# Attention's raw queries loaded six steps ahead of their rounding, into three buffers of their low parts

## The chip, the cores and the metric

The kernel runs on one core of a Trainium2 chip. The metric is device time in microseconds (us), the median of several runs. A core has five engines with instruction streams of their own: TensorE (PE, with its weight loads as PEld), VectorE (DVE), ScalarE (ACT), GpSimd (POOL) and SyncE (SP), which here issues nearly all DMA transfers. Each engine takes its instructions in the order in which they stand; semaphores make one wait for another.

## The reference, cut to what matters

One layer of a hybrid encoder over 2048 tokens (a 32 x 64 grid) and 16 meta tokens. An input projection feeds two mixers: neighbourhood attention (8 heads of 64, a window of 8 rows x 16 columns, a relative-position bias, 16 keys that all see) and a bidirectional gated DeltaNet (4 heads of 128, chunks). An output projection, a SwiGLU feed-forward and a norm follow.

```
s_grid = einsum('brqhd,brikhd->bhrqik', qg, k_win) + bias      # attention
s_meta = einsum('brqhd,bmhd->bhrqm', qg, km)
p      = softmax(concat([s_grid, s_meta]))
v_new  = u_i - w_i @ state                                     # DeltaNet, chunk by chunk
o_i    = q_i @ state + qk_i @ v_new
state  = state * cd_i + k_i^T @ v_new
h = h + concat([y_na, y_dn]) @ w_out;  h = h + (silu(u @ w_gate) * (u @ w_up)) @ w_down
```

## The kernel before

Phase A (up to about 880 us in the profile) projects and prepares; it writes queries, keys and values to DRAM scratch. Phase B (about 880 to 1300 us) runs attention and the DeltaNet scan side by side. Phase C does the output projection and the feed-forward, and PE is its limit.

Phase B is one loop over steps i (line 1322). A step of attention treats 128 queries of one head; four steps make a slot (32 slots, 128 steps). Beside it stands a step of the scan, `scan_a`, `scan_b`, `scan_c`, with one more scan step in each 16. In step i the code issues the transposes of i-1 (`att_t`, L1134), the scores of i+1 (`att_s`, L1120 and L1121), the values' load of i+4 (`att_v`, L1077) and the output of i-2 (`att_o`, L1148).

PE multiplies in a rounded form, so that a slot's queries are split: `load_q` (L1055) brings the raw queries (128 x 512, 256 KB, as two transfers of 64 partitions) into `qr`; `split` rounds them on ACT to `q1` (L1068), and POOL writes the rest `qr - q1` to `q2` (L1070). Both are multiplied with the keys. Slot n is first used by `att_s(4n)`, in step 4n-1. Its split is issued in step 4n-3 (`i % 4 == 1`). `qr` has one buffer, so the load, in step 4n-6 (`i % 4 == 2`), waits until POOL has finished the split of slot n-1, of step 4n-7. `q1` and `q2` have two buffers each.

What else SP loads in phase B: the bias `b` of a slot (L1062, in step 4n-5, two buffers, 336 to 672 KB), the scan's chunks `w<-dx` (L1179, 1 MB each) and `xq` (L1182, 512 KB), the keys `k` (L1047, 544 KB each), later the gates `z` (L1254) and the output weights `yu` (L1388). All are in one queue, q1. ACT also does the softmax (L1127), the copies `pT` of transposed scores (L1136) and the scan's `vn` (L1213 to L1217) and `oacc` (L1245), in one stream with the rounding of queries.

A scheduler sets each engine's order from the program, with times of its own for each instruction, and `tc.issue_after` holds the loads behind the last load of values. So an edit of a buffer count or of a step number moves instructions of other kinds as well.

Of the kernel before, what the change touches and what calls it, by code (L numbers as in the profile page):

```python
# [8 lines left out]
F32 = mybir.dt.float32  # L9
F32R = mybir.dt.float32r  # L10
# [6 lines left out]
P = 128  # L17
# [1001 lines left out]
def attention_slots():  # L1019

    slots = [Slot(2 * hp + a, [(C, 0, 4)]) for hp in range(3) for C in range(4) for a in range(2)]
    for R in (2, 0):
        slots += [Slot(6 + a, [(C, R, R + 2), (C + 1, R, R + 2)]) for C in (0, 2) for a in range(2)]
    return slots


def attention_loads(tc, S, es, rel):

    nc = tc.nc
    kp = es.enter_context(tc.tile_pool(name="b_k", bufs=2, reuse_waits="tile"))  # L1030
    vp = es.enter_context(tc.tile_pool(name="b_v", bufs=LV + 3, reuse_waits="tile"))
    A = Ctx()
    A.slots = attention_slots()
    A.kp, A.pools = kp, [kp, kp]
    A.tiles, A.last, A.keys = {}, None, {}

    def at(i):

        s = A.slots[i // 4]
        R, C, o = s.tiles[i % 4]  # L1040
        nch = 3 if CN[C] == 24 or R == 0 else 4
        return s, R, C, o, KWIN[R][0], KWIN[R][1], nch, KWIN[R][1] * CN[C] // nch

    def load_k(h):
        kk = A.pools[h % 3].tile([P, 34, 64], F32R, name=f"k{h % 3}", bufs=1)
        for l in range(2):
            nc.sync.dma_start(kk[l * 64:(l + 1) * 64].rearrange("p r c -> p (r c)").bitcast(F32), S.kx[h // 2, l, h % 2])  # L1047
        A.keys[h] = kk

    def load_q(n):  # L1050
        s = A.slots[n]
        s.qr = kp.tile([P, 512], F32, name="qr", bufs=1)
        C, R0, R1 = s.segs[0]
        for d in range(2):
            nc.sync.dma_start(s.qr[d * 64:(d + 1) * 64].rearrange("p (f n) -> p f n", f=len(s.segs)),  # L1055
                              S.qx[s.h, C:C + len(s.segs), :, R0 * P:R1 * P].rearrange("f d n -> d f n"))

    def load(n):
        s = A.slots[n]
        s.b = kp.tile([P, 1624], F32, name="b")  # L1060
        for o, src, n in s.bias:
            nc.sync.dma_start(s.b[:, o:o + n], rel[s.h, :, src:src + n])  # L1062

    def split(n):
        s = A.slots[n]
        s.q1 = kp.tile([P, 512], F32R, name="q1")
        s.q2 = kp.tile([P, 512], F32R, name="q2")
        nc.scalar.copy(s.q1, s.qr)  # L1068
        for c in (slice(0, 256), slice(256, 512)):
            nc.gpsimd.tensor_tensor(s.q2[:, c], s.qr[:, c], s.q1[:, c], ALU.subtract)  # L1070

    def load_v(i):
        s, R, C, o, k0, nr, nch, w = at(i)
        t = A.tiles[i] = Ctx()
        t.v = vp.tile([P, 4, 64], F32, name="v")
        src = S.vx[C][s.h].rearrange("r c d -> (r c) d")[k0 * CN[C]:(k0 + nr) * CN[C]]
        A.last = nc.sync.dma_start(t.v[0:w, 0:nch], src.rearrange("(p k) d -> p k d", k=nch))  # L1077

    A.at, A.load, A.load_q, A.load_k, A.split, A.v = at, load, load_q, load_k, split, load_v
    load_k(0)  # L1080
    load_q(0)
    load(0)
    split(0)
    load_v(0)
    return A


def phase_b(tc, S, A, W, norm_g, following):
# [4 lines left out]
    with ExitStack() as es:  # L1093
# [18 lines left out]
        def att_s(i):  # L1112
            s, R, C, o, k0, nr, nch, w = att_at(i)
            n = nch * w
            t = tiles[i]
            ps = pa_.tile([P, 512], F32, name="y")
            qs = slice(i % 4 * P, i % 4 * P + P)
            keys = A.keys[s.h][:, k0:k0 + nr, CLO[C]:CLO[C] + CN[C]]
            pv = ps[:, 0:n].rearrange("p (r c) -> p r c", r=nr)
            nc.tensor.matmul(pv, s.q1[:, qs], keys, start=True, stop=False)  # L1120
            nc.tensor.matmul(pv, s.q2[:, qs], keys, start=False, stop=True)  # L1121
            t.sb = ap_.tile([P, 512], F32, name="sb", bufs=3)
            t.mx = ap_.tile([P, 4], F32, name="mx", bufs=6)
            nc.vector.tensor_tensor_reduce(out=t.sb[:, 0:n], in0=ps[:, 0:n], in1=s.b[:, o:o + n], scale=1.0, scalar=-3.0e38,
                                           op0=ALU.add, op1=ALU.max, accum_out=t.mx[:, 0:1])
            nc.gpsimd.tensor_scalar(t.mx[:, 1:2], t.mx[:, 0:1], -1.0, None, op0=ALU.mult)
            nc.scalar.activation(t.sb[:, 0:n], t.sb[:, 0:n], AF.Exp, bias=t.mx[:, 1:2], accum_out=t.mx[:, 2:3])  # L1127

        def att_t(i):
            s, R, C, o, k0, nr, nch, w = att_at(i)  # L1130
            t = tiles[i]
            pt = pa_.tile([P, 4, P], F32, name="y")
            for c in range(nch):
                nc.tensor.transpose(pt[0:w, c], t.sb[:, c:nch * w:nch], S.ident)  # L1134
            t.pT = ap_.tile([P, 4, P], F32, name="pT", bufs=2)
            nc.scalar.copy(t.pT[0:w, 0:nch], pt[0:w, 0:nch])  # L1136
# [30 lines left out]
        def scan_load(s):  # L1167


            cs = (s, 15 - s)  # L1170
            new = [c for c in cs if c not in dxt]
            for c in new:
                dxt[c] = W.tile([P, 4, 4, P], F32, name="w")
            for d in range(2):
                xqt[d, cs[d]] = xp.tile([P, 4, 2, P], F32, name=f"xq{d}")
            for d, c in enumerate(cs):
                if c in new:
                    place[c] = (0, 1, 2, 3) if d == 0 else (3, 0, 1, 2)
                    nc.sync.dma_start(dxt[c], S.dx[c, :, :, d:d + 4].rearrange("h p a i -> p h a i"))  # L1179
                elif s != 8:  # L1180
                    nc.sync.dma_start(dxt[c][:, :, place[c][0]], S.dx[c, :, :, 4 * d].rearrange("h p i -> p h i"))
                nc.sync.dma_start(xqt[d, c], S.xq[d, c].rearrange("h p a i -> p h a i"))  # L1182
# [105 lines left out]
        nq = Pieces()  # L1288
        scan_load(0)
        A.load_q(1)  # L1290
        A.load_k(1)
        for i in range(1, LV):
            att_v(i)
# [2 lines left out]
        def scan_begin(j):  # L1296
            if j % 8 == 0 and j + 8 < N:
                with tc.issue_after(S.last.ins if j == 0 else A.last.ins):
                    scan_load(j // 8 + 1)
            if j < N:  # L1300
                scan_a(j)
# [15 lines left out]
        def scan_middle(j):  # L1317
            if 0 <= j - 1 < N:
                scan_b(j - 1)

        j = 0
        for i in range(N + 4):
            if i % 32 == 8 and i < 96:
                with tc.issue_after(A.last.ins):
                    A.load_k(i // 32 * 2 + 2)
            if i % 32 == 28 and i < 96:
                with tc.issue_after(A.last.ins):
                    A.load_k(i // 32 * 2 + 3)
            if (i == 0 or i % 4 == 3) and i < 120:
                with tc.issue_after(A.last.ins):  # L1330
                    A.load((i + 1) // 4 + 1)
            if i % 4 == 1 and i < 124:
                A.split(i // 4 + 1)
            if i % 4 == 2 and i < 120:
                with tc.issue_after(A.last.ins):
                    A.load_q(i // 4 + 2)
            extra = i % LEAD == LEAD - 1
            steps = list(range(j, min(j + 1 + extra, N + 2)))
            j = min(j + 1 + extra, N + 2)
            if 0 <= i - 1 < N:  # L1340
                att_t(i - 1)
            for k in steps[0:1]:
                scan_begin(k)
            if i + 1 < N:
                if min(j, N) - 5 in done:
                    with tc.issue_after(done[min(j, N) - 5].ins):
                        att_s(i + 1)
                else:
                    att_s(i + 1)
            if i + LV < N:  # L1350
                att_v(i + LV)
            for k in steps[0:1]:
                scan_middle(k)
            if 0 <= i - 2 < N:
                att_o(i - 2)
            for k in steps[0:1]:
                scan_end(k)
            for k in steps[1:]:
                scan_begin(k)
                scan_middle(k)  # L1360
                scan_end(k)
            nq.step(3 if j < N + 2 else 6)
            if i == SCANNED:
                assert j == N + 2
                nq.drain()
                es2.close()
                following()
# [538 lines left out]
```

## Time and profile before

| | us |
|---|---|
| median of 3 runs (lowest to highest) | 2893.03 (2889.85 to 2894.18) |
| the profiled execution's own time | 2883.66 |
| its span | 2881.9 |
| PE busy in the span | 2740.7 (95%) |
| phase B, about | 880 to 1300 |

PE is busy for 95% of the span, but not evenly: in phase A's end and in phase B it stands still now and then, and the clock granted to it (1.00 is 2.4 GHz, 0.50 is 1.2 GHz) falls in these places. The "busy" of PE is modelled at its ends; a bracket behind an instruction in the timeline gives the idle time just ahead of it and what ended it. A DMA share of 1.0 means that the 16 DMA engines are all occupied.

### The profile page before, as it was taken

The page shows a single profiled execution, that of the slowest core. Times are in us where ns is not written, and L with a number is a line of the kernel's source. Part 1 is how long each engine was busy: PE and PEld are TensorE (multiplying, and loading weights), DVE is VectorE, ACT ScalarE, POOL GpSimd, SP SyncE. Part 2 cuts the span into 40 slices and gives each one's busy share as a digit, 9 for nine tenths or more (in the row PEclk, how much of TensorE's full clock was granted, in tenths as well). Part 3 has the DMA queues.
Part 4 walks back from the last instruction along what each step waited for, and adds up shares of the span by engine and source line. Part 5 has one row for each costly group of instructions (what it writes and reads, how often), then busy time and mean ns, then how long its engine had stood idle before and what let it go on. Part 6 is the DMA issues. An engine that isn't in the chain of part 4 may idle for free.

```text
span 2881.9 us, 45992 instructions
## 1 busy us (share of the span) xinstructions
PE 2740.7 (95%) x16364; PEld 2400.2 (83%) x16364; DVE 1758.0 (61%) x3916; ACT 1170.4 (41%) x2741; POOL 744.4 (26%) x809
## 2 busy tenths in 40 slices
PE   8999988988988999979999999999999999999998
PEld 8999988988888988878887888877887888888886
DVE  5897467895643556764567566554548556654354
ACT  4652333652415667752334333243434333233342
POOL 2253353341511212221134322300104322220010
PEclk9999999999989999989999999999999999999999
DMA  4675654565769888985534222246353222225452
GB/s 151 189 205 142 163 165 135 172 179 172 211 159 287 265 229 254 291 281 156 176 126 163 81 88 80 81 131 246 128 176 119 80 86 88 74 95 201 143 179 70
DMA packets 385220, 462.15 MB, mean 160 GB/s; under 512 B 93492, under 2 KB 277133, under 8 KB 383423
## 3 DMA queue, kind: packets, MB, share of 16 engines
q1 hardware_dynamic: 383262, 452.92, 51.5%
q0 software_dynamic: 1728, 6.29, 0.6%
q8 instruction: 130, 2.13, 0.3%
q14 instruction: 100, 0.81, 0.1%
HBM read 329.95 MB, written 136.95 MB: 162 GB/s over the span
## 4 chain that ended last, share of the span: by engine, by line
PE 54%; DMA 3%; DVE 2%; ACT 0%; issue 0%; POOL 0%; SPq 0%; DVEq 0%; ACTq 0%; POOLq 0%
PE pg L1609 24%; PE pg L1685 8%; PE pd L1469 6%; PE pd L1685 4%; PE tp L1685 4%; PE pd L1609 4%; DMA rt<-ut 1%; DMA z<-zx 1%; PE y L1148 1%; DMA k<-kx 0%; PE tp L1495 0%; PE tp L1416 0%; DMA qr<-qx 0%; DVE w L1453 0%; PE y L1134 0%
## 5 line engine op out<-in xcount | busy, mean ns | idle before, releaser
L405 PE MATMUL acc<-uh,wf 128*128 128x384 f32 (+5 forms) x1920 | 469.2, 328 | 2.3 <-ACT uh L342 1.1
L1609 PE MATMUL pg<-T,w 128*128 128x512 f32 x1584 | 393.2, 397 | 2.6 <-ACT T L1452 1.4
L1453 DVE TENSOR_TENSOR w<-rw,w 128x512 fp32r<-128x512 f32 x308 | 241.1, 785 | 251.4 <-ACT w L1452 250.5
L1609 PE MATMUL pg<-B,w 128*128 128x512 f32 x1584 | 388.6, 398 | 3.6 <-ACT B L1452 3.0
L1452 ACT CAST w<-rw 128x512 fp32r<-128x512 f32 x308 | 190.2, 620 | 485.5 <-PE tp L1685 253.4
L1609 PEld LDWEIGHTS pg<-B,w 128*128 128x128 f32 x1584 | 299.1, 189 | 77.9 <-ACT B L1452 3.9
L1609 PEld LDWEIGHTS pg<-T,w 128*128 128x128 f32 x1584 | 298.0, 188 | 76.4 <-ACT T L1452 1.8
L405 PEld LDWEIGHTS acc<-uh,wf 128*128 128x128 f32 x1920 | 339.5, 192 | 4.9 <-ACT uh L342 1.2
L405 PE MATMUL acc<-ul,wf 128*128 128x384 f32 (+5 forms) x960 | 312.3, 325 | 0.0
L1557 POOL TENSOR_TENSOR s<-rw 128x512 f32<-128x512 f32 x88 | 120.4, 1369 | 548.0 <-DMA rw<-in_w_gate_dram 297.8
L1685 PE MATMUL pg<-w,hT 128*128 128x512 f32 x1056 | 260.8, 395 | 1.2 <-ACT hT L1452 1.1
L1685 PEld LDWEIGHTS pg<-w,hT 128*128 128x128 f32 x1056 | 198.1, 188 | 50.0 <-ACT hT L1452 1.5
L429 PE MATMUL acc<-wn,uh 128*128 128x256 f32 (+3 forms) x1056 | 210.7, 298 | 8.5 <-DVE vs L473 8.2
L1453 DVE TENSOR_TENSOR w<-s,w 128x512 fp32r<-128x512 f32 x176 | 131.6, 750 | 137.9 <-ACT w L1452 136.8
L1452 ACT CAST w<-s 128x512 fp32r<-128x512 f32 x176 | 108.5, 620 | 233.5 <-PE pg L1609 138.4
L405 PEld LDWEIGHTS acc<-ul,wf 128*128 128x128 f32 x960 | 184.3, 192 | 1.0 <-DVE ul L343 0.2
L429 PEld LDWEIGHTS acc<-wn,uh 128*128 128x128 f32 (+1 forms) x1056 | 173.3, 197 | 11.4 <-DVE vs L473 8.7
L429 PE MATMUL acc<-wn,ul 128*128 128x256 f32 (+3 forms) x528 | 158.0, 299 | 2.3 <-DVE rx_i L58 2.3
L1469 PE MATMUL pd<-w,yh 128*128 128x512 f32 x512 | 160.0, 394 | 0.0
L499 DVE SCALAR_TENSOR_TENSOR ct<-cr,cw,ct 128x1024 f32<-128x1024 f32 (+1 forms) x96 | 136.4, 1426 | 37.7 <-ACT ct L497 36.5
L242 POOL TENSOR_TENSOR wf<-raw,wf 128x512 fp32r<-128x512 f32 x80 | 117.7, 1486 | 154.9 <-ACT wf L241 131.6
L1623 DVE TENSOR_TENSOR eg<-pg,eg 128x512 f32<-128x512 f32 x110 | 75.9, 690 | 106.4 <-PE pg L1609 106.3
(359 smaller groups left out, 5305.0 us busy)
## 6 DMA issues: line engine op xcount, KB each, us to landing
rw<-in_w_down_dram SPq DMA_DIRECT2D x88, 512.0 KB
w<-dx SPq DMA_DIRECT2D x24, 1024.0 KB
rw<-in_w_gate_dram SPq DMA_DIRECT2D x44, 512.0 KB
rw<-in_w_up_dram SPq DMA_DIRECT2D x44, 512.0 KB
hd<-eg SPq DMA_DIRECT2D x88, 256.0 KB
s<-hd SPq DMA_DIRECT2D x88, 256.0 KB
raw<-in_w_feat_dram SPq DMA_DIRECT2D x80, 256.0 KB
xq<-xq SPq DMA_DIRECT2D x32, 512.0 KB
```

Of the source, the lines that this page charges most:

```text
L242: nc.gpsimd.tensor_tensor(lo, raw, hi, ALU.subtract)
L405: nc.tensor.matmul(ps[:, 0:c1 - c0], hl[:, a, k, :], (U.h, U.l)[l][ci][:, k, c0:c1], start=(i == 0), stop=(i == 23))
L429: nc.tensor.matmul(ps[0:np_, 0:n], (U.h, U.l)[l][ci][:, k, off:off + np_], hl[:, a, k, 0:n], start=(i == 0), stop=(i == 23))
L499: nc.vector.scalar_tensor_tensor(tt, raw[:, j:j + T], cw[:, b, j:j + 1], tt, op0=ALU.mult, op1=ALU.add)
L1148: nc.tensor.matmul(po, t.pT[0:w, c], t.v[0:w, c], start=(c == 0), stop=(c == nch - 1))
L1452: nc.scalar.copy(dst_h, src)
L1453: eng.tensor_tensor(dst_l, src, dst_h, ALU.subtract)
L1469: nc.tensor.matmul(ps, (yh, yl)[a][:, k], wo[k][:, b, cs], start=(i == 0), stop=(i == 23))
L1557: nc.gpsimd.tensor_tensor(s, p, q, op)
L1609: nc.tensor.matmul(ps, w[:, a, k], t[:, b, k], start=(k == 0 and (a, b) == (0, 0)), stop=(k == 3 and a == 1))
L1623: nc.vector.tensor_tensor(dst, ps, x0, ALU.add)
L1685: nc.tensor.matmul(acc[j][hf], hk[f][:, a, j * P:(j + 1) * P], wk[f][hf][:, b], start=(f == 0 and i == 0), stop=(f == NFF - 1 and i == 2))
```

## The change

`qr` loses its own buffer. The raw queries go to the buffer of the low parts, `q2`, which has three buffers in place of two (the memory stays the same), and POOL subtracts in place. The load of slot n moves from step 4n-6 to step 4n-9, six steps ahead of the split in place of three. It now waits until PE has made the last product with `q2` of slot n-3, `att_s(4n-9)`, issued in step 4n-10. Slot 2 is loaded before the loop as well.

```diff
     def load_q(n):
         s = A.slots[n]
-        s.qr = kp.tile([P, 512], F32, name="qr", bufs=1)
+        s.q2 = kp.tile([P, 512], F32R, name="q2", bufs=3)
+        s.qr = s.q2.bitcast(F32)
...
         s.q1 = kp.tile([P, 512], F32R, name="q1")
-        s.q2 = kp.tile([P, 512], F32R, name="q2")
         nc.scalar.copy(s.q1, s.qr)
...
         A.load_q(1)
+        A.load_q(2)
         A.load_k(1)
...
-            if i % 4 == 2 and i < 120:
+            if i % 4 == 3 and i < 116:
                 with tc.issue_after(A.last.ins):
-                    A.load_q(i // 4 + 2)
+                    A.load_q(i // 4 + 3)
```

SP's order around the fourth load of keys, before: `b` is the bias, `qr` the raw queries (the first here are slot 9's), `v` values, `k` keys, `w` and `xq` the scan's chunks.

```order
570 L1062 DMA b<-in_rel_dram 128x1008
571 L1077 DMA v<-vx_62 104x192
572 L1047 DMA k_11464<-kx 64x2176 x2
573 L1077 DMA v<-vx_59 96x192
574 L1077 DMA v<-vx_59 128x192
575 L1055 DMA qr<-qx 64x512 x2
576 L1077 DMA v<-vx_59 128x192
577 L1179 DMA w<-dx 128x4x512 x2
578 L1062 DMA b<-in_rel_dram 128x1008
579 L1077 DMA v<-vx_59 104x192
```

The same place now; `q` is the buffer of low parts that takes the raw queries of slots 10 and 11.

```order
569 L1056 DMA q_11418<-qx 64x512
570 L1063 DMA b<-in_rel_dram 128x1008
571 L1056 DMA q_11418<-qx 64x512
572 L1077 DMA v<-vx_62 104x192
573 L1047 DMA k_11459<-kx 64x2176 x2
574 L1077 DMA v<-vx_59 96x192
575 L1077 DMA v<-vx_59 128x192 x2
576 L1179 DMA w<-dx 128x4x512 x2
577 L1056 DMA q_11582<-qx 64x512
578 L1063 DMA b<-in_rel_dram 128x1008
579 L1056 DMA q_11582<-qx 64x512
```

The queries stand on both sides of a bias now, one slot and more ahead of where they stood; the keys, the values, the bias and the chunks keep their order among themselves.

ACT's order around the rounding of slot 4, before: the rounding stands behind the last exponential (128 x 416) ahead of its slot.

```order
687 L1136 COPY pT<-y 128x512
688 L1127 ACTIVATE sb,mx<-sb,mx 128x416
689 L1213 ACTIVATE vn<-z,kd 128x128
690 L1217 COPY vn<-z 128x128
691 L1068 CAST q_10799<-qr 128x512
692 L1136 COPY pT<-y 128x512
```

The same rounding now:

```order
669 L1217 COPY vn<-z 128x128
670 L1068 CAST q_10798<-q_10546 128x512
671 L1127 ACTIVATE sb,mx<-sb,mx 128x416
672 L1245 COPY oacc<-z 128x128
673 L1136 COPY pT<-y 128x512
674 L1213 ACTIVATE vn<-z,bkd 128x128
```

It stands five exponentials, so five steps of attention, further ahead. In most other slots the rounding stood as far ahead in the kernel before.

## Rows read from the trace of the kernel before

**Rows 1.** The page: span, busy time of each engine, the chunks' transfers
```profile
span 2881.9 us, 45992 instructions
PE 2740.7 (95%) x16364; PEld 2400.2 (83%) x16364; DVE 1758.0 (61%) x3916; ACT 1170.4 (41%) x2741; POOL 744.4 (26%) x809
...
w<-dx SPq DMA_DIRECT2D x24, 1024.0 KB
```

**Rows 2.** Windows: phase B, a quiet stretch, two parts of B
```profile
core 0: us, PE busy (x) PEld busy (x) DVE busy (x) ACT busy (x) POOL busy (x), PEclk, DMA share, GB/s
880.00:1300.00 420.00, 371.29 (x2826) 358.78 (x2825) 253.80 (x1038) 270.12 (x873) 93.73 (x221) 0.91 0.90 270
957.00:977.00 20.00, 20.00 (x173) 19.86 (x172) 10.80 (x46) 14.55 (x47) 4.31 (x12) 1.00 1.03 312
940.00:1180.00 240.00, 221.57 (x1779) 216.70 (x1778) 141.97 (x594) 161.56 (x534) 54.16 (x132) 0.95 0.87 251
1180.00:1256.00 76.00, 66.57 (x515) 63.55 (x513) 61.77 (x260) 57.69 (x191) 19.21 (x39) 0.93 1.02 321
```

**Rows 3.** Tile qr, 880 to 1300 us: who waited for it
```profile
  ACT q L1068: 51.1, 12
```

**Rows 4.** PE's timeline: three of seven stalls, and slot 25's first scores
```profile
930.00 0.69 PE L1120 MATMUL y<-k,q 128*128 128x384 f32 x1 [2.98 <-ACT q L1068]
983.36 0.80 PE L1232 MATMUL z<-S,w 128*128 128x128 f32 x2 [4.26 <-ACT vn L1217]
1195.88 0.67 PE L1120 MATMUL y<-k,q 128*128 128x384 f32 x1
1281.50 0.91 PE L1134 MATMUL y<-ident,sb 128*128 128x128 f32 x3 [6.19 <-ACT sb L1127]
```

**Rows 5.** ACT's timeline at two of these places
```profile
982.27 0.62 ACT L1068 CAST q<-qr 128x512 fp32r<-128x512 f32 x1 [4.44 <-DMA qr<-qx]
983.06 0.25 ACT L1217 COPY vn<-z 128x128 f32<-128x128 f32 x1
...
1193.33 0.62 ACT L1068 CAST q<-qr 128x512 fp32r<-128x512 f32 x1 [8.74 <-DMA qr<-qx]
```

**Rows 6.** Windows: the seven stretches from a stall to the clock's return
```profile
926.00:937.00 11.00, 8.02 (x42) 7.63 (x41) 3.27 (x11) 3.90 (x12) 1.83 (x4) 0.69 0.99 336
978.00:988.00 10.00, 5.74 (x31) 5.53 (x31) 2.80 (x13) 4.16 (x14) 1.80 (x4) 0.66 1.05 345
1020.00:1033.00 13.00, 7.87 (x43) 7.39 (x42) 2.95 (x12) 4.63 (x14) 1.76 (x4) 0.74 1.03 282
1079.00:1087.00 8.00, 4.16 (x23) 3.93 (x23) 2.52 (x12) 4.12 (x14) 1.60 (x3) 0.79 0.92 265
1115.00:1125.00 10.00, 6.83 (x34) 6.27 (x34) 4.21 (x18) 4.75 (x15) 1.74 (x4) 0.66 0.93 283
1186.00:1199.00 13.00, 7.18 (x36) 6.69 (x34) 6.35 (x21) 5.67 (x16) 3.21 (x6) 0.62 1.07 315
1275.00:1289.00 14.00, 7.81 (x41) 7.65 (x40) 6.21 (x20) 3.62 (x9) 6.22 (x11) 0.63 0.68 195
```

**Rows 7.** SP's timeline: loads of queries, chunks and bias
```profile
922.87 0.54 SPq L1062 DMA_DIRECT2D b<-in_rel_dram  x1
...
973.36 1.09 SPq L1055 DMA_DIRECT2D qr<-qx  x2
...
976.83 2.07 SPq L1179 DMA_DIRECT2D w<-dx  x2
...
1182.12 0.61 SPq L1055 DMA_DIRECT2D qr<-qx  x1
...
1188.91 0.33 SPq L1062 DMA_DIRECT2D b<-in_rel_dram  x1
```

**Rows 8.** SP's own waits, 840 to 1320 us
```profile
SPq L1062 <- DVE R L1201: 10.0, 10, 2.9
SPq L1055 <- POOL mx L1126: 4.7, 5, 2.0
```

**Rows 9.** DVE, 880 to 1300 us: the add of the bias, by line
```profile
L1124 DVE CUSTOM_DVE_ANT_0 sb<-y,b 128x384 f32<-128x384 f32 (+4 forms) x128 | 72.6, 570 | 26.8 <-PE y L1121 19.4 <-issue 3.6 <-POOL q L1070 0.9
```

## The prediction

> **What bounds the kernel now.** I read the page first: PE is busy for 2740.7 of 2881.9 us [rows 1]. So only stretches in which PE stands still, or runs at half clock, have anything to give, and I looked for those with the windows. In 880 to 1300 us PE is busy for 371.29 of 420 us at a mean clock of 0.91, while the DMA engines are at 0.90 of their time [rows 2]. This is where the queries are loaded; phase C behind it is bound by PE. Then the tile `qr`: inside these 420 us ACT waits 12 times, 51.1 us together, for the raw queries of a slot [rows 3]. Whether that reaches PE is seen on PE's own timeline. At 930.00 PE waits 2.98 us for the rounded queries themselves. At 983.36 it waits 4.26 us, and for the scan's `vn`, which has nothing to do with queries [rows 4]: ACT stood 4.44 us in front of the rounding at 982.27, and `vn` is behind it in ACT's stream [rows 5]. So a late query stops the softmax and the scan, steps before its slot is used. Seven such places stop PE: in slots 4, 9, 12, 17, 20, 25 and 31.
>
> Each costs more than its idle time. After it the granted clock is 0.50 for some microseconds, which is the level of 1.2 GHz. What a place costs is read from its window: length, less its matmuls divided by the rate of a quiet stretch, which is 173 in 20 us, or 8.65 in a us, at a clock of 1.00 [rows 2]. The seven windows [rows 6] give 11 - 42/8.65 = 6.1; 10 - 31/8.65 = 6.4; 13 - 43/8.65 = 8.0; 8 - 23/8.65 = 5.3; 10 - 34/8.65 = 6.1; 13 - 36/8.65 = 8.8; 14 - 41/8.65 = 9.3. Together 50.0 us. That is the whole of what earlier queries can bring here.
>
> **The change part by part.** *The load moves three steps ahead.* Phase B's 2826 matmuls over 128 steps are 22 to a step, and 22/8.65 = 2.5 us is a quiet step [rows 2], so the load gets some 7.6 us more. From the issue to the rounding it took 982.27 - 973.36 = 8.9 us in slot 9 and 1193.33 - 1182.12 = 11.2 us in slot 25 [rows 5, 7]; ACT had stood there for 4.44 and 8.74 us of these. Moved by 7.6 us, the first is in time with 3 us to spare, and the second is late by about 1 us. For slot 25 there is more: its load stood behind the keys, and now stands ahead of them, as the order around the fourth load of keys shows in another slot. So I count the waits for queries as gone, or small. In slot 4 the rounding itself has moved five exponentials ahead, so that there the added time is mostly taken back by an earlier deadline; its load, too, stands four loads of values further ahead in SP's order than it did, and I count it as in time.
>
> *The new wait.* The load now waits on SP for PE's product of slot n-3. Behind it on SP stand a bias, values and chunks, and PE and DVE wait for those. But the bias beside it waits for DVE's add in the same attention step 4n-9, which comes after that product. So the new wait ends first, and holds SP for no longer than it would be held: 0 us. The bias's own waits show the size, 10.0 us in 10 times [rows 8], none of them followed by a wait of DVE (below). The old wait, for POOL, goes: 4.7 us in 5 times, SP's alone, worth 0 by itself. If PE's product came after the bias's release, one step would be lost to all loads behind it; the price of that is a rival below.
>
> *Instructions.* The two loads, the rounding and the two subtractions remain, as many and as long. POOL now writes in the buffer that it reads; the trace has no row of that. The bounds are 0 and the time of one product of POOL that others wait for, and no engine but PE waits for it, a slot ahead: 0 taken. Three loads of 256 KB are under way or held where one was; bytes and buffers are the same in sum.
>
> *What is late next.* The queue is. In 880 to 1300 us it moved 270 GB/s x 420 us = 113.4 MB. With every engine occupied (1.03) it moved 312 GB/s, so those bytes take 363 us: 57 us less than now, for all of the phase. But the room isn't where the stalls are: 940 to 1180 us has 60.2 MB, 193 us at 312 GB/s, so 47 us free; 1180 to 1256 us ran at 321 GB/s and a share of 1.02 and has none [rows 2]. Four of the seven windows are full (shares of 0.99, 1.05, 1.03 and 1.07), three are not (0.92, 0.93, 0.68) [rows 6].
>
> The transfer that would be late next is the bias. It is issued four steps ahead of its use, about 10.2 us, and is larger than the queries. Its slack today is made by the stalls: in slot 4 it is issued at 922.87 and PE starts on the slot at 930.00, 7.1 us later; in slot 25 at 1188.91 and 1195.88, 7.0 us [rows 4, 7]. Queries took 8.9 to 11.2 us in a full queue. That no DVE add ever waits for a DMA [rows 9] says only that the queries were later still.
>
> The sum. Windows that aren't full: slots 17 and 20 in whole, 5.3 + 6.1 = 11.4. Slot 31 lies at the end of attention, where no scan is left to fill PE and the steps wait for each other; of its 9.3 I take two thirds, 6. The four full windows (6.1 + 6.4 + 8.0 + 8.8 = 29.3): between nothing (the bias takes over) and all, I take a third, 10, since two of them (slots 4 and 25) have a bias just behind and two (9 and 12) have a bias issued well before its use. 11.4 + 6 + 10 = 27 us. The profiled execution took 2883.66 us, so 2856 in its terms; it lies 9.4 us under the median of the runs shown, 2893.03, from which I take the 27: **2866 us**.
>
> The Trainium skill speaks for more: "DMA: Bandwidth & Descriptors", Specifications, puts HBM's limit for one core at about 358 GB/s. By that figure the 113.4 MB would need 317 us (an estimate of that page), the queue would be no limit, and all 50 us would come. The rows disagree, since 312 and 321 GB/s went with shares above 1.0 [rows 2]; I go by them.
>
> **The rivals.**
> *All of it comes:* 2893 - 50 = 2843. For it: every one of the seven stalls ends with a query, and no other transfer is seen to be waited for. Against it: the full queue in four of them.
>
> *The wait only changes its name:* with earlier queries the bias, the values or a chunk stops DVE and PE at the same places, and only the 11.4 us of slots 17 and 20 come, or half of it, since steps that run faster fill the queue there too: 2882 to 2887. For it: 7 us between issue and use of the bias in slots 4 and 25. Against it: in the other slots the bias has a step more than the queries had.
>
> *Slower:* the bias is late at the twelve pairs of chunks. The order shows two chunks of 1 MB (2.1 MB, 6.7 us at 312 GB/s) directly ahead of query, bias, query, so that a bias meets a full queue there. Queries took 8.9 to 11.2 us in a full queue, and a bias of 504 KB is 0.25 MB more, 0.8 us: some 10 to 12 us, up to 2 us after its use at 10.2. With the clock's loss, about 3 us in each of the seven windows (6.1 less 2.98 idle in the first), that is 5 us, and for the twelve pairs [rows 1] 60; less the 50 gained, 2903. It decides from a latency of the bias of 10.2 us on. Against it: the chunks stood directly ahead of a bias before as well [rows 7], and no add waited for one.
>
> *The change doesn't do what it says:* SP comes to the loads no sooner, since its place is set by the loads of values ahead of it, and the queries still arrive after ACT. The roundings stand up to five steps ahead of their use in ACT's stream, so a part of this is likely; all of it would be 2893. Against it: SP's order has them three loads of values further ahead.
>
> **How the numbers follow.** Forecast, around 2866: 0.50, its own range 2854 to 2879. All of it: 0.17. The wait changes its name: 0.16, half of it below the bound. Nothing comes: 0.08. Slower: 0.09. A measurement of this kernel tells about 0.2% from no change, 5.8 us. Faster: 0.50 + 0.17 + 0.11 = 0.78. Same: 0.05 + 0.08 = 0.13. Slower: 0.09. The range reaches to 2845, nearly to the whole of the gain, and to 2888, the end of the second rival; it leaves about 0.2 out, most of it on the slow side and below 2845.
>
> **What would show it.** In the profile of the changed kernel ACT's wait for the queries' transfer falls from 51 us to under 10; PE has no idle time of over 2 us for ACT's `vn`, `sb` or `oacc` behind a rounding between 940 and 1180 us; the clock's mean in phase B rises from 0.91 to 0.95 or more; the DMA rate of phase B rises from 270 to about 288 GB/s (113.4 MB in some 393 us); and DVE's add shows a DMA, the bias, among its releasers. If PE's stalls are gone and the bias is no releaser, the gain was cut too far; if ACT's wait stays above 30 us, the move of SP's loads was the wrong step; if the stalls stay with other names, the queue was the limit.

## The result, and the profile after

| | before | changed |
|---|---|---|
| median, us (lowest to highest) | 2891.44 (2888.75 to 2894.18) | 2866.62 (2864.26 to 2869.15) |
| ratio, 95% interval | | 0.9923 [0.9903, 0.9943] |
| the profiled execution | 2883.66 | 2866.91 |

The forecast was 2866. But the two profiled executions differ by only 16.75 us: that of before lay 7.8 us under its median, that of the change at its own. In a later comparison of the two the change stood at 2866.18 and 0.9927 [0.9903, 0.9951], the kernel before at 2886.15. So the change is worth 20 to 25 us.

The page, first lines, answering to [rows 1]; PE is busy for 9.9 us less:
```profile
span 2865.1 us, 46004 instructions
...
PE 2730.8 (95%) x16364; PEld 2391.9 (83%) x16364; DVE 1765.7 (62%) x3916; ACT 1170.9 (41%) x2741; POOL 742.8 (26%) x809
```

Windows of the changed kernel, three stretches of [rows 2] and a further one of 20 us (columns as there):
```profile
880.00:1300.00 420.00, 374.28 (x2904) 360.05 (x2903) 263.17 (x1057) 272.58 (x879) 92.83 (x220) 0.95 0.93 273
940.00:1180.00 240.00, 224.50 (x1825) 219.27 (x1825) 152.93 (x631) 164.61 (x546) 54.52 (x136) 0.97 0.95 267
1180.00:1256.00 76.00, 70.91 (x555) 68.33 (x554) 62.11 (x262) 62.62 (x202) 21.51 (x46) 0.96 1.02 332
1160.00:1180.00 20.00, 14.38 (x113) 13.29 (x112) 13.32 (x66) 9.85 (x34) 2.66 (x8) 0.99 1.04 238
```
The granted clock rose from 0.91 to 0.95, and between 940 and 1180 us the DMA share from 0.87 to 0.95: PE made 1825 products there in place of 1779, and the queue is fuller.

Tile `q`, who waited (the answer to [rows 3]: 51.1 us in 12 times):
```profile
  DMA q<-qx: 29.1, 11
```
The wait is smaller, not gone. PE's timeline, every stall of over 2 us from 900 us on (beside [rows 4]):
```profile
929.20 0.49 PE L1199 MATMUL z<-S,w 128*128 128x128 f32 x2 [2.23 <-ACT oacc L1245]
...
987.16 0.80 PE L1199 MATMUL z<-S,w 128*128 128x128 f32 x2 [4.47 <-ACT oacc L1245]
...
1088.05 0.91 PE L1134 MATMUL y<-ident,sb 128*128 128x128 f32 x3 [2.75 <-ACT sb L1127]
...
1177.76 0.85 PE L1148 MATMUL y<-v,pT 128*128 128x64 f32 x6 [2.92 <-DMA v<-vx]
...
1277.83 2.07 PE L1470 MATMUL pd<-w,yh 128*128 128x512 f32 x4 [13.74 <-ACT yh L1419]
```
Before there were seven, 29.8 us together; now there are four inside attention, 12.4 us, and a new one behind it, 13.74 us. ACT's timeline at the first, the second and the last:
```profile
928.36 0.62 ACT L1068 CAST q<-q 128x512 fp32r<-128x512 f32 x1 [5.72 <-DMA q<-qx]
...
986.32 0.62 ACT L1068 CAST q<-q 128x512 fp32r<-128x512 f32 x1 [6.52 <-DMA q<-qx]
986.84 0.26 ACT L1245 COPY oacc<-z 128x128 f32<-128x128 f32 x1
...
1277.19 1.07 ACT L1419 CAST yh<-tp 128x512 fp32r<-128x512 f32 x2 [16.28 <-DVE z L1281]
```
The first three lines are the picture of before again ([rows 5]): ACT stands in front of a rounding, and the scan's copy behind it is late for PE. The stall at 1088.05 is not of this kind, since no rounding waited there. POOL stood in front of the gates `z` of a norm; the softmax's `mx` came behind them, and ACT and PE waited for it:
```profile
1085.68 1.40 POOL L1256 TENSOR_TENSOR z<-z,ng 128x256 f32<-128x256 f32 x2 [5.65 <-DMA z<-zx]
...
1087.29 0.61 ACT L1127 ACTIVATE sb<-sb,mx 128x384 f32<-128x384 f32 x1 [3.54 <-POOL mx L1126]
```
And the one at 1177.76 waits for values. So two of the four stalls end with a query, one with gates, one with values. The four windows, by the measure of [rows 6]:
```profile
925.00:934.00 9.00, 6.77 (x43) 6.33 (x42) 2.77 (x10) 4.26 (x13) 1.83 (x4) 0.81 1.04 267
984.00:994.00 10.00, 6.84 (x39) 6.84 (x40) 3.37 (x14) 5.71 (x20) 1.82 (x4) 0.66 0.98 277
1084.00:1092.00 8.00, 5.25 (x30) 5.06 (x29) 2.10 (x9) 4.71 (x18) 4.73 (x9) 0.71 1.08 331
1174.00:1184.00 10.00, 7.03 (x45) 6.52 (x44) 3.11 (x14) 3.43 (x13) 1.58 (x3) 0.83 1.00 287
```
Length less matmuls by 8.65 is 4.0 + 5.5 + 4.5 + 4.8 = 18.8 us, against 50.0 before. So by this measure 31.2 us were gained inside attention, and 13.7 of idle time came behind it. The balance, 17.5, is near the 16.75 between the profiled executions. (The products behind the new wait are slow as well: the first eight output products take 4.3 us, 2.4 before, so that the loss is some 2 us more than the idle time.)

The loss: the last gates (norm of chunk pair 15), in the timelines of DVE, POOL and SP:
```profile
1273.53 3.57 DVE L1281 SCALAR_TENSOR_TENSOR z<-oacc,of,z 128x128 f32<-128x128 f32 x8 [9.94 <-POOL z L1256]
...
1272.78 1.40 POOL L1256 TENSOR_TENSOR z<-z,ng 128x256 f32<-128x256 f32 x2 [11.03 <-DMA yu<-yo]
...
1268.68 0.41 SPq L1254 DMA_DIRECT2D z<-zx  x1
...
1270.93 0.34 SPq L1254 DMA_DIRECT2D z<-zx  x1
```
PE's last product of attention starts at 1262.0 us, where it started at 1309.0 before. But the loads of the last `z` are issued at 1268.68 and 1270.93, since `z` has two buffers and SP has other loads ahead; POOL, DVE, ACT and PE follow one another from there, and the first output product starts at 1277.83 (1294.4 before), 17 us sooner. The 47 us are not like for like: before, the output products had begun ahead of attention's last 26 products and stood among them; now all of attention comes first.

Where did the longer lead go? SP's timeline at slot 10's load:
```profile
971.77 0.45 SPq L1056 DMA_DIRECT2D q<-qx  x1
973.93 0.35 SPq L1063 DMA_DIRECT2D b<-in_rel_dram  x1
976.20 0.45 SPq L1056 DMA_DIRECT2D q<-qx  x1
```
The second half goes out 4.4 us after the first, a bias between them, and 10.1 us ahead of the end of ACT's wait at 986.32. From the starts of all loads and roundings of slots 4 to 31 the medians are: from the second half's issue to the rounding 6.2 us before, 9.45 now; from the rounding to the slot's first scores 8.85 before, 12.35 now. So of the 7.6 us planned, the transfer got 3.3; 3.5 went to roundings that themselves stand further ahead. What SP waits for ahead of the queries' loads now (us, times, longest), 840 to 1320 us:
```profile
SPq L1056 <- DMA xq<-xq: 10.9, 6, 2.9
SPq L1056 <- DMA k<-kx: 6.2, 4, 2.1
SPq L1056 <- DMA b<-in_rel_dram: 5.8, 6, 2.0
SPq L1056 <- PE y L1121: 2.7, 5, 1.2
SPq L1056 <- POOL q L1070: 2.5, 4, 1.2
SPq L1056 <- POOL mx L1126: 2.2, 3, 1.3
```
The new wait for PE's product is the fourth line, and small. The last two say that SP still waits for POOL, 4.7 us as before [rows 8]; why, the record doesn't show. The first three are transfers still under way: all of SP's waits for a DMA, 880 to 1300 us, sum to 121.8 us (before 90.2).

DVE's add of the bias, the answer to [rows 9]:
```profile
L1124 DVE CUSTOM_DVE_ANT_0 sb<-y,b 128x384 f32<-128x384 f32 (+4 forms) x128 | 72.8, 570 | 22.4 <-PE y L1121 11.9 <-POOL q L1070 4.4 <-issue 3.6
```
The bias is not among the three releasers that the line names; the view of all waits has it once, with 0.5 us. The 4.4 us for POOL's `q` (0.9 before) are a single wait.

### The profile page after: what moved, and what is told of

The parts are those of the page before. It is cut to its first block, busy times and chain, and to the rows that moved or that the text cites. A ratio compares the mean times of both kernels' runs of the same rounds, so it can differ in the third digit from the quotient of the medians.

```text
span 2865.1 us, 46004 instructions
## 1 busy us (share of the span) xinstructions
PE 2730.8 (95%) x16364; PEld 2391.9 (83%) x16364; DVE 1765.7 (62%) x3916; ACT 1170.9 (41%) x2741; POOL 742.8 (26%) x809
## 4 chain that ended last, share of the span: by engine, by line
PE 69%; DMA 11%; DVE 10%; issue 4%; POOL 3%; ACT 2%; SPq 2%; DVEq 0%; POOLq 0%; ACTq 0%
PE pg L1610 25%; PE pg L1686 8%; PE pd L1470 6%; PE acc L405 5%; PE pd L1686 4%; PE tp L1686 4%; PE pd L1610 4%; PE acc L429 3%; DVE ct L499 2%; PE y L1148 2%; DMA q<-qx 1%; DMA w<-dx 1%; DMA xq<-xq 1%; DVE tl L166 1%; DVE yl L167 1%
## 5 line engine op out<-in xcount | busy, mean ns | idle before, releaser
L429 PEld LDWEIGHTS acc<-wn,uh 128*128 128x128 f32 (+1 forms) x1056 | 173.2, 197 | 13.7 <-DVE vs L473 10.8
L1470 PE MATMUL pd<-w,yh 128*128 128x512 f32 x512 | 161.2, 397 | 13.7 <-ACT yh L1419 13.7
```

The source lines that it names most:

```text
L429: nc.tensor.matmul(ps[0:np_, 0:n], (U.h, U.l)[l][ci][:, k, off:off + np_], hl[:, a, k, 0:n], start=(i == 0), stop=(i == 23))
L1470: nc.tensor.matmul(ps, (yh, yl)[a][:, k], wo[k][:, b, cs], start=(i == 0), stop=(i == 23))
```

## The experiments

Three theories stood against each other: the gain comes from the lead of the load; it comes from the buffers, which free the rounding and its place in ACT's order; and what remains is held by the queue's bytes or by its order. Times are compared with the kernel before in the same comparison: 2886.47 us for the first four, 2886.04 for the next four, 2886.15 for the last three.

**Buffers alone** (on the kernel before):
```diff
-        s.qr = kp.tile([P, 512], F32, name="qr", bufs=1)
+        s.q2 = kp.tile([P, 512], F32R, name="q2", bufs=3)
+        s.qr = s.q2.bitcast(F32)
...
-        s.q2 = kp.tile([P, 512], F32R, name="q2")
```


> The three shared buffers alone: the raw queries go into the buffer of the low parts, but are loaded in step 4n-6 as in the kernel before, three steps ahead of the rounding. Theory (the lead of the load is what pays): the load still has about 8 us to the rounding, ACT's wait for queries in phase B stays at 40 to 55 us, and the time is that of the kernel before, 2886 to 2893 us; only the start of phase B, where slot 1's load no longer waits for POOL, may give 2 to 3 us. Rival A (the second wait that went, for POOL's subtraction on one buffer, is what pays): ACT's wait falls to about 29 us as in the changed kernel and the time is about 2867 us. Rival B (any new order by the scheduler does it): somewhere between, with PE's stalls in other places but ACT's wait for queries not smaller.


Measured: 2874.68 us, 0.9957 [0.9940, 0.9973], 11.8 us less. In its trace:
```profile
ACT q L1068 <- DMA q<-qx: 35.3, 12, 5.8
```
The time lies between the theory's and rival A's, and ACT's wait, at 35.3 us, is smaller than the theory and rival B had it. About half of the gain comes without any step of lead, although PE waits ahead of the output products here already (9.79 us). The issue-to-rounding median is 6.7 us, hardly longer than before (6.2). What did change is the rounding's place: in the kernel before, eight slots (4, 5 and 25 to 30) are rounded less than 3 us ahead of their first scores, here two, in the changed kernel none. The load's wait for POOL is gone as well. Which of the two brings the 11.8 us was not separated: of the seven stalls before, only those of slots 4 and 25 had so late a rounding.

**Five steps instead of six** (on the changed kernel, slot 2 not loaded ahead of the loop):
```diff
-            if i % 4 == 3 and i < 116:
+            if i % 4 == 0 and i < 120:
                 with tc.issue_after(A.last.ins):
-                    A.load_q(i // 4 + 3)
+                    A.load_q(i // 4 + 2)
```


> Three shared buffers, load in step 4n-8, five steps ahead of the rounding: a dose between three and six. Theory (lead): ACT's wait for queries between 29 and 51 us, about 33 to 40, and a time of 2870 to 2880 us. Rival A (buffers): 2867 us, no dose. Rival B (order by the scheduler): no relation to the dose, anything from 2860 to 2895 us.


Measured: 2864.56 us, 0.9920 [0.9901, 0.9940], the same as the change and faster than the theory had it; ACT's wait 37.1 us in 12 times, as the theory had it. Two steps of lead bring the other half (the intervals just touch), the third nothing that can be measured. The wait's sum is a poor guide: 37.1 here and 29.1 there go with the same time.

**Without the queries' loads** (the kernel before; slot 0's raw queries are used for all slots, 31 loads are left out):
```diff
     def load_q(n):
         s = A.slots[n]
+        if n:
+            s.qr = A.slots[0].qr
+            return
```


> The kernel before, with raw queries loaded for slot 0 alone; every later slot rounds those of slot 0 (this leaves 31 loads of 256 KB out, 8 MB of the phase's 113 MB). ACT then never waits for queries. Theory (the changed kernel's remaining 29 us of query waits cost little, since its end of phase B is set by the last norm's chain of gates): attention ends some 50 us earlier than before, but the first product of the output projection comes no earlier than about 1270 us, and the time is 2850 to 2866 us, within 0.6% of the changed kernel. Rival (the queries' waits are still the price, 50 us in all as the windows gave): 2843 us or less, with the whole gain in the end.


Measured: 2834.91 us, 0.9827 [0.9801, 0.9854], 51.6 us less; the rival was right. The seven windows had given 50.0. Its windows:
```profile
880.00:1300.00 420.00, 402.75 (x3093) 387.68 (x3093) 281.39 (x1089) 279.92 (x894) 102.19 (x225) 0.96 0.86 269
...
1200.00:1220.00 20.00, 20.00 (x172) 19.76 (x170) 18.57 (x76) 17.03 (x59) 8.40 (x15) 1.00 1.03 360
```
Nor does PE wait behind attention there: the first output product starts at 1248.3. So that wait isn't a floor. But this edit also takes 8 MB out of the queue, and the last gates are loaded at 1237.87 us here; that the sum is so near 50.0 doesn't prove each window's price.

**The last gates in another buffer** (on the changed kernel):
```diff
+            if s == 15:
+                last = xp.tile([P, 4, 2, P], F32, name="xq0").rearrange("p h a i -> p (h a i)")
-            for c in (s, 15 - s):
-                z = sp.tile([P, 4, P], F32, name="z", bufs=2)
+            for j, c in enumerate((s, 15 - s)):
+                if s == 15:
+                    z = last[:, j * 512:j * 512 + 512].rearrange("p (h d) -> p h d", h=4)
+                else:
+                    z = sp.tile([P, 4, P], F32, name="z", bufs=2)
```


> The changed kernel, but the last norm's gates (z, step 15) go into a freed buffer of the scan's xq, so that their load need not wait until norm 14's results are stored. Theory (PE's 13.7 us of idle time at 1264 to 1278 us is the price at which attention's gain is given back, and this chain is its cause): that idle time falls to under 6 us and the time falls by 6 to 12 us to about 2857 us. Rival C (the output projection waits for its inputs yu anyway, 2 to 3 us later): the idle time only changes its name and the time falls by less than 3 us.


Measured: 2862.41 us, 0.9912 [0.9895, 0.9929], about 4 us under the change, within the intervals. PE's timeline there shows no wait ahead of the output product:
```profile
1274.90 2.05 PE L1475 MATMUL pd<-w,yh 128*128 128x512 f32 x4
```
The idle time is gone, as the theory had it, but the gain lies between the theory's 6 to 12 us and rival C's 3. The product starts only 2.9 us sooner than in the change (1277.83). Two things hide the rest. Phase B itself began later in this execution, its first scores at 885.9 us in place of 879.6; the changed kernel profiled once more (below) began at 886.1, so that this need not be the edit's work. And from its first scores to its last outputs attention took 388.8 us in place of 382.4. From the first scores to the first output product it is 389.0 us here and 398.2 in the change (396.6 once more): 8 to 9 us of the phase are saved.

**Without most of the bias, changed kernel and kernel before** (the bias of slots 0 and 1 serves all later ones):
```diff
     def load(n):
         s = A.slots[n]
+        if n >= 2:
+            s.b = A.slots[n - 2].b
+            return
         s.b = kp.tile([P, 1624], F32, name="b")
-        for o, src, n in s.bias:
-            nc.sync.dma_start(s.b[:, o:o + n], rel[s.h, :, src:src + n])
+        nc.sync.dma_start(s.b, rel[s.h, :, 0:1624])
```


> The changed kernel with the bias loaded for slots 0 and 1 only and used again by all others: it leaves out 30 slots' bias transfers, some 15 to 19 MB of the 113 MB of phase B, and computes with the wrong bias. Theory (the queue is full, so that a query loaded six steps ahead is late all the same): with those bytes gone ScalarE's wait for queries falls from 29 us to under 10 and the time to about 2840 (2833 to 2848), nearly the 2834.9 of the kernel without query loads. Rival (the loads are late because of their place in SyncE's stream and of what SyncE waits for, not because of the bytes): ScalarE's wait stays above 20 us, the time at 2858 to 2867. Second rival (the bias's own waits on SyncE hold the loads up): the same fall as in the theory, but in the stretches with a DMA share under 0.9 too.

> The kernel before with the bias loaded for slots 0 and 1 only: the same bytes are left out. Theory (queue): the wait of ScalarE for queries falls from 51 us to 15 to 30, since the one buffer and the short lead remain, and the time from about 2888 to 2855 to 2868. Rival (lead and buffer alone decide): the wait stays above 40 us and the time above 2878.


Measured: 2839.22 us, 0.9833 [0.9815, 0.9852] on the changed kernel; 2863.51 us, 0.9915 [0.9890, 0.9940] on the kernel before. The changed kernel without the bias, its window and ACT's wait:
```profile
880.00:1300.00 420.00, 393.76 (x3023) 377.95 (x3022) 275.61 (x1084) 279.45 (x890) 98.83 (x224) 0.96 0.80 235
...
ACT q L1070 <- DMA q<-qx: 3.0, 1, 3.0
```
The kernel before without it:
```profile
880.00:1300.00 420.00, 384.11 (x2946) 369.85 (x2945) 261.20 (x1058) 272.54 (x880) 94.60 (x221) 0.95 0.77 228
...
ACT q L1070 <- DMA qr<-qx: 29.8, 12, 6.2
```

| us, median | all bias loaded | two slots' bias |
|---|---|---|
| before | 2886 | 2863.5 |
| changed | 2866 | 2839.2 |

(The changed kernel's 2866 is from the last comparison, where the kernel before took 2886.15.)

Both results lie where the queue theory had them. The four corners nearly add: the change is worth 20 us in the full queue and 24 in the relieved one, the bias's bytes 23 and 27. In the same 420 us the queue of the changed kernel moves 16 MB less ((273 - 235) GB/s x 420 us). So there are two causes, but the second is not only that queries are late. In the changed kernel phase B begins at 879.6 us with and without the bias. Its last attention output starts at 1262.0 and 1256.1 us, 5.9 sooner; its first output product starts at 1277.83 with the bias, and without it at
```profile
1256.28 1.20 PE L1472 MATMUL pd<-w,yh 128*128 128x512 f32 x4
```
with no wait ahead of it, 21.6 us sooner. So some 16 of the 25 us between the two profiled executions are the wait for the last gates, whose last load is issued at 1236.36 us here and at 1270.93 in the change. ACT's waits for queries fell from 29.1 to 3.0 us, and attention became only 5.9 us shorter. The bias's own waits on SP go with its bytes; that rival was not separated.

The kernel before waits 29.8 us for queries without the bias, at a DMA share of 0.77. That mean doesn't clear the queue, since the two longest of these waits (6.22 us up to 1011.38, 5.12 us up to 1179.44) fall into full stretches:
```profile
1001.00:1011.00 10.00, 8.01 (x68) 7.76 (x66) 3.19 (x12) 3.50 (x12) 0.42 (x2) 1.00 1.07 253
...
1170.00:1179.00 9.00, 6.86 (x45) 6.41 (x43) 6.73 (x32) 2.47 (x8) 0.21 (x1) 0.82 1.04 246
```

**A queue of its own for the queries** (on the changed kernel):
```diff
-            nc.sync.dma_start(s.qr[d * 64:(d + 1) * 64]...
+            (nc.gpsimd if n else nc.sync).dma_start(s.qr[d * 64:(d + 1) * 64]...
...
-                with tc.issue_after(A.last.ins):
-                    A.load_q(i // 4 + 3)
+                A.load_q(i // 4 + 3)
```


> The changed kernel with the raw queries' loads (slots 1 to 31) issued by GpSimd in a queue of its own instead of SyncE's, at the same step. The bytes are the same. Theory (all 16 DMA engines are full, whatever the queue): ScalarE's wait stays at 20 to 35 us and the time within 2860 to 2870. Rival (the queries stand behind chunks and keys in one queue, served in order): the wait falls below 10 us, and the time to 2840 to 2850; then values or the bias, now behind nothing new, should show no later. A third way: GpSimd is held by its wait for TensorE's product and its subtractions come late, 2870 or more.


Measured: 2862.46 us, 0.9921 [0.9906, 0.9936]: the change's ratio. No rounding waits for a transfer any more. But the waits view of DVE and PE has other names now, and GpSimd issues the loads itself (last line, its groups):
```profile
DVE sb L1124 <- DMA b<-in_rel_dram: 12.1, 6, 3.8
...
PE z L1209 <- DMA xq<-xq: 6.2, 2, 4.1
...
PE z L1199 <- DMA w<-dx: 4.9, 4, 1.5
...
L1056 POOL DMA_DIRECT2D q<-qx x58 | 33.4, 575 | 37.9 <-PE y L1121 20.0 <-PE z L1209 8.2 <-PE z L1199 8.0
```
The rival was right that the queries stood behind others, and the theory that it doesn't help: with the same bytes the bias (12.1 us, 0.5 in the change), the chunks and `xq` come late in their place. POOL also stands 37.9 us in front of the loads, waiting for PE; how much of the lost gain is due to that was not separated.

**Two edits together: five steps, and the last gates' buffer** (the diffs are those above):


> Two edits of earlier runs together: three buffers with the load five steps ahead of the rounding, and the last gates' z in a chunk's freed buffer. If their small gains add (2864.6 and 2862.4 beside 2866.6 for the change), 2858 to 2861; if the handover absorbs one of them, 2862 to 2866.


Measured: 2856.03 us, 0.9899 [0.9879, 0.9919], under both ranges.

**GpSimd's queue, and the last gates' buffer** (also the diffs above):


> Raw queries in GpSimd's own queue and the last gates' z in a chunk's freed buffer, on the changed kernel. Theory (phase B is held by the bytes of its transfers, so that an edit of their order only changes which transfer is late): no more than the better of the two parts, 2856 to 2863, with the bias still a releaser of VectorE's add. Rival (the handover is a loss of its own, worth the 6 us that TensorE still waited there with GpSimd's queue): 2850 to 2856.


Measured: 2852.99 us, 0.9879 [0.9855, 0.9902]; the rival was right. The first output product, from PE's timeline:
```profile
1265.17 1.17 PE L1474 MATMUL pd<-w,yh 128*128 128x512 f32 x4
```
It starts 7.7 us sooner than with GpSimd's queue alone (1272.91), 4.8 counted from phase B's first scores, and behind no wait. Here the last outputs of attention came at 1274.9 us, beside output products that had begun already.

**The change again, and five steps with the other buffer again**, in the same comparison as the one before:


> The changed kernel itself, on the same chip and beside the same runs of the kernel before as the two others, so that small differences between versions can be told: 0.992 of the kernel before, 2862 to 2868. If it stands within 3 us of the version with five steps and the other z buffer, that version's 10 us were the chip's.

> Three buffers, the load five steps ahead of the rounding and z in a chunk's freed buffer, once more beside the change: 2853 to 2860 and a ratio of 0.988 to 0.992 to the kernel before. If it is 0.992 or above, it is no better than the change.


Measured: 2866.18 us, 0.9927 [0.9903, 0.9951], and 2857.70 us, 0.9887 [0.9863, 0.9912]. In that comparison the two versions with the last gates' buffer lie 8 and 13 us below the change, every run of theirs under every run of the change; which of the two is better can't be told. The change's profile shows the 14 us wait behind attention once more (14.12 us at 1282.67).

## Why the prediction was right, and where it wasn't

*What bounds the kernel, 50.0 us in seven windows:* right in its size; taking the queries away gave 51.6, with 8 MB less in the queue. But not "every one of the seven stalls ends with a query". The one in slot 25, which ended at 1191.45 with a result of DVE, stood behind gates as well (kernel before; the second line's view names a load of values, but the product reads the gates):
```profile
1189.73 1.05 DVE L1281 SCALAR_TENSOR_TENSOR z<-oacc,of,z 128x128 f32<-128x128 f32 x2 [4.80 <-POOL z L1256]
...
1188.97 1.40 POOL L1256 TENSOR_TENSOR z<-z,ng 128x256 f32<-128x256 f32 x2 [6.14 <-DMA v<-vx]
```
ACT's wait for the query ended only at 1193.33. Two late transfers lay over each other there, and 8.8 of the 50.0 us were put down to one.

*"So the load gets some 7.6 us more":* this is the step that failed, and with it "I count the waits for queries as gone, or small". SP's order did put the loads ahead, but an order isn't a time: SP waits longer for transfers under way, the second half follows behind a bias, and the scheduler moved the roundings ahead as well. The transfer got 3.3 us more at the median, and 29.1 us of ACT's waits stayed. They cost PE less than that: two stalls still end with a query, 4.0 and 5.5 us by their windows. By the prediction's own sign (above 10, below 30) that lies between right and "the move of SP's loads was the wrong step". The sign that no stall of over 2 us would follow a rounding between 940 and 1180 us failed at 987.16.

*Slot 4, "mostly taken back by an earlier deadline":* half right. Slot 4 stalls no more, its rounding now 14.0 us ahead of its first scores (0.7 before). But slot 5's rounding waits 5.72 us at 928.36, and PE behind it 2.23: 4.0 us by its window in place of 6.1. That in most other slots the rounding stood as far ahead before overlooked eight slots with under 3 us. What the buffers bring by themselves, 11.8 us, was no term of the sum, which spoke of the lead alone.

*The new wait on PE's product at 0 us:* right, 2.7 us in 5 times. *"The old wait, for POOL, goes":* not by SP's view, which has 4.7 us for POOL as before. *POOL's subtraction in place at 0:* its median is 728 ns (737 before). That "no engine but PE waits for it" isn't what the view says: [rows 9] names it as the end of a wait of DVE, 0.9 us, now 4.4; whether this reached PE was not tested.

*"The transfer that would be late next is the bias":* not in the changed kernel, where it costs DVE 0.5 us; the values do at 1177.76. It is the bias once the queries are out of its way, in GpSimd's queue (12.1 us).

*The queue as the limit:* right as a cause of what remains, since leaving out the bias brings 27 us, more than half of it at the handover to the output products. Inside attention 31.2 us came, not 27; the thirds that the sum took of the full windows were a choice. Sorting the windows into full and not full couldn't tell which would go: they begin with PE's stall, when the late transfer is nearly through. While the queries of slots 17 and 20 were under way, whose windows counted as not full, the engines were occupied (kernel before):
```profile
1073.00:1082.00 9.00, 6.66 (x58) 6.47 (x56) 2.97 (x12) 2.95 (x10) 0.42 (x2) 1.00 0.98 221
1108.00:1117.00 9.00, 7.60 (x63) 7.31 (x62) 8.07 (x43) 3.89 (x13) 0.62 (x3) 1.00 1.04 228
```
And the ceiling of 312 GB/s was no ceiling: [rows 6] has 345.

*The missing term:* the handover. Attention that ends sooner meets the last gates, whose loads come when a buffer and SP are free. The sum had no term for it. It is 13.7 us of PE's wait, worth 4 to 10 us by the experiments that gave the last gates another buffer. In the terms of the profiled execution the sum gave 2856; 2866.91 came. So the median was met to a microsecond by luck: 31.2 in place of 27 us inside attention, the loss at the handover against it, and a profiled execution of before that lay 9.4 us under the median shown with it.

*The signs:* the clock rose to 0.95 as said; the DMA rate went to 273, not 288 GB/s. The rival "the wait only changes its name" holds for the handover, where 13.7 of the 31.2 us went again, for the stalls by gates and values at 1088.05 and 1177.76, and for GpSimd's queue. In the chances, 0.11 of that rival's 0.16 were counted as faster, where "half of it below the bound" makes 0.08.

## What to carry to other kernels

A load moved ahead in program order gains less than the steps say: measure from its issue to its use, since the queue's own waits and the instruction that uses it move too. A buffer can be worth as much as a lead (11.8 us here), and whether by the freed load or by the scheduler's new order has to be tested. Read the queue's share while the transfer is under way; a mean over the phase, or a window that begins with the stall, misses it. A late transfer stops whatever stands behind its first user in an in-order engine: queries on ACT, gates on POOL and DVE. When a stage is shortened by tens of microseconds, look at what its successor needs and when those loads can start. And compare stages by their length, since two profiled executions of the same changed kernel began phase B 6.5 us apart.

## What the runs showed of the hardware

All 16 DMA engines occupied isn't one rate. The share was 1.04 at 238 GB/s in the changed kernel (1160 to 1180 us) and 1.03 at 360 GB/s without the queries' loads (1200 to 1220 us), both in the windows above. The prediction's ceiling of 312 GB/s was one mix of transfers, no limit of the chip. The Trainium skill's "DMA: Bandwidth & Descriptors", Specifications, puts HBM's limit for one core at about 358 GB/s: the second window lies at it, the first shows that a full queue can be far below it, and ten microseconds of the kernel before lie above it, so that the measurement decides:
```profile
1227.00:1237.00 10.00, 10.00 (x85) 9.82 (x85) 8.98 (x47) 7.29 (x28) 1.60 (x5) 1.00 1.06 383
```

The loads that GpSimd issued occupied it for 575 ns each (58 of them, 33.4 us), and it had waited 37.9 us for PE ahead of them. That its small steps for the softmax came later by this isn't shown: ACT's wait for them was 52.2 us with GpSimd's queue, 48.4 with that queue and the other buffer, and 37.1 to 50.3 in the versions without it.
